# A decoder layer with a mixture of experts on one core: weights laid out in the order of their loads

## The chip, the core and the metric

The kernel runs on one core of a Trainium2 chip. The metric is the device time of one execution in microseconds; the median of three executions of the kernel before is 1303.94 us (1302.9 to 1305.6).

## What is computed

One decoder layer for 256 tokens of width 1024 in float32, then a final RMSNorm. Cut to what matters:

```
mod = silu(c) @ ada_w + ada_b                       # 1024 -> 6 x 1024
h = modulate(rmsnorm(x, norm1_g), sh1, sc1)
z = h @ w_in                                        # 1024 -> 6144
rnn_x, rnn_gate, sg_u, sg_v, g_rnn, g_sg = split(z)
y_rnn = rg_lru(conv(rnn_x), lru_wa, lru_wx, ...) * gelu(rnn_gate)
y_sg = spatial_gating(gelu(sg_u), gelu(sg_v), sg_ws, ...)
m = sigmoid(g_rnn) * (y_rnn @ w_br_rnn) + sigmoid(g_sg) * (y_sg @ w_br_sg)
x = x + gt1 * (m @ w_out)
h = modulate(rmsnorm(x, norm2_g), sh2, sc2)
# 32 experts, each token goes to 4 of them
gate, up = split(h[tok] @ w_gu[e] + b_gu[e])        # 1024 -> 2 x 1024
act = (clip(up) + 1) * gate * sigmoid(1.702 * gate)
x = x + gt2 * sum_e weight * (act @ w_down[e] + b_down[e])
out = rmsnorm(x, final_g)
```

## The kernel before

SBUF holds a pool of 24 slots of 128 partitions by 2048 float32 (8 KB per partition, 1 MiB each). Every weight passes through one of them. `want` (line 64) puts a load on a list, `stream`, in the order in which the weights are used; `pump` (line 72) issues loads from its head on SyncE's queue as long as a slot is free; `give` (line 95) frees a slot when its content has been used, and calls `pump`. So the order of the loads is fixed, and a load is late only when its slot is.

The mixer part comes first, its steps written out by hand. `ada_rows` (line 337) multiplies the first 2048 columns of ada_w, in six `PIECES`, on TensorE or VectorE; `ada_cols` and `modulate` turn the result into h. Each weight tile of w_in, w_br_rnn, w_br_sg and w_out is split by `split` (line 258) into a high part (ScalarE or VectorE) and a low part (GpSimd or VectorE), and multiplied by TensorE in three products. A weight tile is gathered from its matrix by `blocks` (line 113): rows k*128 + p of some columns, so that a partition's 8 KB come in runs of 512 columns (2 KB) or 1024 columns (4 KB); those of ada_w at the start are cut into runs of 128 or 256 columns (512 B or 1 KB), with up to four DMAs for a slot. `small_loads` (line 190) brings sg_ws and the diagonal blocks of lru_wa and lru_wx; the tile wab that takes these blocks is cleared ahead by GpSimd (line 188). GpSimd's next work is the identity matrix for the transposes (line 221).

Then the 32 experts run one after another (line 1166). Of each, eight loads of w_gu (128 rows of 2048 columns, 8 KB per partition in one run) and four of w_down (two blocks of 128 rows of 1024 columns, so two runs of 4 KB per partition) are streamed, 12 MiB per expert. TensorE gathers the tokens of the next expert, multiplies by w_gu (`up_products`, line 915) and w_down (`down`, line 935), and adds the outcome to x. `w_down` of the last expert is cut at column 384 of each half (WA) and loaded by 16 DMAs. Where an expert has more than 64 tokens, a branch (line 1228) does the rest. [...]

```
def pump():
    while at[0] < len(stream) and (left[0] or stream[at[0]][3]):
def give():
    left[0] += 1
    pump()
nc.tensor.addr_align(bass.FETCH_BLOCK_INSTRUCTIONS, offset=FETCH_SLOT, max_nops=0)
```

Of the kernel before, what the change touches and what calls it, by code (L numbers as in the profile page):

```python
# [14 lines left out]
D = 1024  # L15
# [7 lines left out]
WA = 384  # L23
BIG = 3.0e38

FETCH_SLOT = 252

LIMIT = 7.0
ALPHA = 1.702
# [7 lines left out]
PIECES = ((0,), (1,), (2, 3), (4, 5), (6,), (7,))  # L37
ROWS_ON_PE = (0, 1, 4, 5)

C_C, C_AB, C_G1, C_CW, C_CB, C_BA, C_BX, C_LAM, C_LNG, C_LNB = 0, 8, 56, 64, 96, 104, 112, 120, 128, 136  # L40
N_COLS = 144

R_G2, R_BS, R_FG = 0, 1, 2


@with_exitstack
def layer(ctx: ExitStack, tc: tile.TileContext, x, cols, rows, ada_w, ada_b, w_in, lru_wa, lru_wx,
          sg_ws, w_br_rnn, w_br_sg, w_out, w_router, b_router, w_gu, b_gu, w_down, b_down, out):
# [12 lines left out]

    stream, at, where, left, waiting, R, hooks = [], [0], {}, [NS - NU], [], {}, {}

    def want(key, src, shape, into=None):
        stream.append((key, src, shape, into))

    def new(name, dt=F32):
        assert left[0] > 0, name
# [1 line left out]
        return slots.tile([128, 2048], dt, name=name, tag="slot")  # L70

    def pump():
        while at[0] < len(stream) and (left[0] or stream[at[0]][3]):
            key, src, shape, into = stream[at[0]]
            at[0] += 1
            if into:
                w = where[into][:, 1024:]
            else:
                w = where[key] = new("_".join(str(k) for k in key))
            if len(shape) == 3:  # L80
                dst = w.rearrange("p (k a c) -> p k a c", k=shape[0], a=shape[1])
# [40 lines left out]
    for g in groups:
        for h in range(2):
            late.append((g, h, blocks(w_in, 4 * h, 4 * h + 4, col0[g], col0[g] + 512), (4, 512)))
    for nm, w in (("br", w_br_rnn), ("bs", w_br_sg)):
        for hf in range(2):
            for h in range(2):
                late.append((nm + "ab"[hf], h, blocks(w, 4 * h, 4 * h + 4, hf * 512, hf * 512 + 512), (4, 512)))
    for q in range(4):
        late.append(("out", q, blocks(w_out, 2 * q, 2 * q + 2, 0, D), (2, 1024)))  # L130
    chunks += [(g, h, shp) for g, h, src, shp in late]
    a1_src = ada_w[:, :2 * D].rearrange("(k p) (a c) -> p k a c", p=128, a=2)
    for i, kbs in enumerate(PIECES):
        n = len(kbs)
        for j in range(n):
            want(("a1", i, j), a1_src[:, j * 4:j * 4 + 8 // n, :, kbs[0] * 128:(kbs[-1] + 1) * 128], (8 // n, 2, 128 * n))
        p = kbs[0] // 2
        for kb in kbs:
            if n == 2:
                if kb % 2 == 0:  # L140
                    want(("w", p), blocks(w_in, kb, kb + 2, 0, D), (2, 1024))
            else:
                want(("w", p, "x")[:2 + kb % 2], blocks(w_in, kb, kb + 1, 0, D), (1, 1024), into=("w", p) if kb % 2 else None)
        if kbs[-1] % 2:
            want(("w", 4 + p // 2, "ga")[:2 + p % 2], blocks(w_in, 2 * p, 2 * p + 2, col0["ga"], col0["ga"] + 512),
                 (2, 512), into=("w", 4 + p // 2) if p % 2 else None)
    ada_at = {i: n for n, i in enumerate(ADA_STEPS)}
    for i in range(6, 4 + len(late) + 2):
        if i < 4 + len(late):
            want(("w", i), *late[i - 4][2:])  # L150
        if i - 4 in ada_at:
            part, kb = divmod(ada_at[i - 4], 8)
            want(("a2", ada_at[i - 4]), blocks(ada_w, kb, kb + 1, 2048 * (1 + part), 2048 * (2 + part)), (1, 2048))
# [12 lines left out]

    xv = view(new("x"), TB)
# [17 lines left out]
    wab = view(R["wab"], 16)  # L185
    rw = R["ws"][:, :1024]
    wr = selX.rearrange("p (k e) -> p k e", k=KB)
    nc.gpsimd.memset(R["wab"], 0.0)

    def small_loads():  # L190
        nc.sync.dma_start(R["ws"][0:1, 1024:], rows[R_BS:R_BS + 1])
        nc.sync.dma_start(brow, b_router)
        for h in range(2):
            nc.sync.dma_start(wsn[h], sg_ws[4 * h:4 * h + 4].rearrange("g t s -> t g s"))
        for a, w in enumerate((lru_wa, lru_wx)):
            wr_ = w.rearrange("(c h) i j -> h i c j", h=2)
            for h in range(2):
# [397 lines left out]


    def load_biases():
        bex = R["h2"][:, :1536]
        for r in range(2):
            for h in range(2):  # L600
                dst = bex[r * 64 + h * 32:r * 64 + (h + 1) * 32]
                nc.sync.dma_start(dst[:, :1024].rearrange("e (a j) -> e a j", a=2),
                                  b_gu.rearrange("e (a h j) -> e h a j", a=2, h=2)[:, h])
                nc.sync.dma_start(dst[:, 1024:], b_down[:, h * 512:(h + 1) * 512])

    def split_biases():
        bex, brs = R["h2"][:, :1536], R["brs"][:, :1536]
# [11 lines left out]
    def merge_s(hf, banks):  # L619
        for j in range(2):  # L620
# [467 lines left out]
    def rare(e):  # L1088
# [30 lines left out]
            mm(BX[h], two[:, h * 32 + e:h * 32 + e + 1].to_broadcast([128, 128]), brs[:, 1024:1536], True, False)  # L1119
        for kb in range(KB):  # L1120
            for h in range(2):
                nc.gpsimd.dma_start(wt2[n % 2], w_down[e, kb * 128:(kb + 1) * 128, h * 512:(h + 1) * 512])
# [181 lines left out]
def _layout(v):  # L1304

    import numpy as np

    v = {k: np.asarray(a) for k, a in v.items()}

    def col(a):  # L1310
        return a.reshape(-1, 128).T

    cols = np.concatenate([col(v[n].reshape(-1)) for n in
                           ("c", "ada_b", "norm1_g", "conv_w", "conv_b", "lru_ba", "lru_bx", "lru_lam",
                            "sg_ln_g", "sg_ln_b")], axis=1)
    rows = np.concatenate([v[n].reshape(1, D) for n in ("norm2_g", "sg_bs", "final_g")], axis=0)
    return {
        "x": v["x"][0], "cols": cols, "rows": rows, "ada_w": v["ada_w"][0], "ada_b": v["ada_b"],
        "w_in": v["w_in"][0], "lru_wa": v["lru_wa"][0], "lru_wx": v["lru_wx"][0], "sg_ws": v["sg_ws"][0],
        "w_br_rnn": v["w_br_rnn"][0], "w_br_sg": v["w_br_sg"][0], "w_out": v["w_out"][0],  # L1320
        "w_router": v["w_router"][0], "b_router": v["b_router"], "w_gu": v["w_gu"][0], "b_gu": v["b_gu"][0],
        "w_down": v["w_down"][0], "b_down": v["b_down"][0],
    }


# [16 lines left out]
```

## Time and profile before

| what | value |
|---|---|
| median of three executions | 1303.94 us (1302.9 to 1305.6) |
| the profiled execution | 1307.48 us, its span 1305.8 us |
| TensorE matmuls busy | 1201.8 us (92% of the span) |
| VectorE, ScalarE, GpSimd busy | 515.2, 244.6, 156.6 us |
| DMA | 472.37 MB in 112112 packets, 77092 of them under 8 KB |
| mean DMA rate over the span | 362 GB/s |
| mean granted TensorE clock | 0.972 |

The time of an execution is what the runs report; the span is the stretch from the first to the last instruction of the profile, and all times in the trace count from its start. TensorE's time is pipelined, so its busy share is not its share of peak. An idle stretch of an engine is put down to the instruction or DMA whose end released it; "issue" stands where the profile shows no releaser.

### The profile page before, as it was taken

Reading aid. Unit: us, or ns where it says so; the run is one execution under the profiler, and the core shown is the slowest. Engines: PE = TensorE matmul, PEld = TensorE weight load, DVE = VectorE, ACT = ScalarE, POOL = GpSimd, SP = SyncE. Lnnn points to the kernel's source line nnn. Section 1 sums busy time; section 2 is a strip of 40 time slices with the busy share of each in tenths; the row PEclk is TensorE's granted clock in tenths of the full one; section 3 lists DMA queues with packets and bytes.
Section 4 is the critical chain, followed back from the end, with each engine's and each line's share of the span. In section 5 each row is a group of like instructions: output and inputs, shape, how many; then the busy total and the mean of one; then the engine's idle time right before and its main releaser. Section 6 shows DMA issues by size and latency. Waiting matters only on the chain. (4 is left out here: it accounts for less than half of the span.)

```text
span 1305.8 us, 17282 instructions
## 1 busy us (share of the span) xinstructions
PE 1201.8 (92%) x6667; PEld 634.1 (49%) x6667; DVE 515.2 (39%) x866; ACT 244.6 (19%) x408; POOL 156.6 (12%) x90
## 2 busy tenths in 40 slices
PE   4798888996999999999999999999999999998996
PEld 4796888985434444434444444333333333333342
DVE  3677998674222232223222323223222222224324
ACT  3264633441200011001000110010000000001102
POOL 2543645543000000000000000000000000000000
PEclk8898989996999999999999999999999999999998
DMA  9995636976799989999999999999999999999981
GB/s 328 332 368 179 218 125 223 400 253 281 316 387 415 409 353 414 414 414 415 415 415 416 415 415 415 415 416 413 414 414 414 410 412 411 413 412 411 416 318 46
DMA packets 112112, 472.37 MB, mean 362 GB/s; under 512 B 10233, under 2 KB 27769, under 8 KB 77092
## 3 DMA queue, kind: packets, MB, share of 16 engines
q1 hardware_dynamic: 111636, 469.61, 90.7%
q8 instruction: 114, 1.87, 0.6%
q14 instruction: 90, 0.74, 0.1%
q0 software_dynamic: 272, 0.16, 0.0%
HBM read 468.68 MB, written 1.05 MB: 360 GB/s over the span
## 5 line engine op out<-in xcount | busy, mean ns | idle before, releaser
L277 PE MATMUL bank<-gu,gv 128*64 128x512 f32 (+1 forms) x2112 | 473.4, 599 | 17.1 <-DMA gu<-in_w_gu 12.4
L277 PEld LDWEIGHTS bank<-gu,gv 128*64 128x64 f32 (+1 forms) x2112 | 143.9, 136 | 307.6 <-issue 251.1
L277 PE MATMUL bank<-dn,tmp 128*64 128x512 f32 (+3 forms) x1120 | 239.0, 576 | 1.1 <-ACT tmp L982 0.3
L1012 DVE TENSOR_TENSOR x<-bank,x 128x512 f32<-128x512 f32 x124 | 79.9, 686 | 151.4 <-PE bank L277 151.4
L277 PEld LDWEIGHTS bank<-selX,h 128*128 128x128 f32 x1024 | 119.3, 195 | 40.7 <-DVE tmp L968 38.0
L277 PE MATMUL bank<-selX,h 128*128 128x128 f32 x1024 | 125.2, 281 | 13.3 <-PEq L1212 11.8
L277 PEld LDWEIGHTS bank<-dn,tmp 128*64 128x64 f32 (+1 forms) x1120 | 71.8, 135 | 132.3 <-issue 118.0
L272 POOL TENSOR_TENSOR parts<-w,parts 128x1024 fp32r<-128x1024 f32 x40 | 117.8, 2955 | 114.6 <-ACT parts L268 82.2
L277 PE MATMUL bank<-hh,parts 128*128 128x256 f32 x640 | 121.2, 300 | 8.1 <-DVE parts L272 4.2
L994 DVE TENSOR_REDUCE wsl<-bank 128x1 f32<-128x256 f32 x33 | 14.0, 425 | 286.5 <-PE bank L993 286.5
L1244 POOL DMA_DIRECT2D selX<-in_rows x4 | 2.2, 544 | 950.8 <-PE bank L277 950.8
L277 PEld LDWEIGHTS bank<-hh,parts 128*128 128x128 f32 x640 | 103.7, 205 | 11.5 <-DVE parts L272 4.6
L969 ACT ACTIVATE tmp<-tmp 128x512 f32<-128x512 f32 (+1 forms) x34 | 20.8, 611 | 466.4 <-DVE tmp L968 466.4
L277 PE MATMUL bank<-hl,parts 128*128 128x256 f32 x320 | 85.2, 297 | 0.0
L268 ACT ACTIVATE parts<-w 128x1024 fp32r<-128x1024 f32 x66 | 67.2, 1052 | 51.2 <-PE bank L277 15.5
L998 DVE SCALAR_TENSOR_TENSOR tmp<-bank,wsl,gt2h 128x512 f32<-128x512 f32 x31 | 23.3, 750 | 130.0 <-PE bank L277 130.0
L1000 ACT ACTIVATE on<-tmp 128x512 fp32r<-128x512 f32 x31 | 19.5, 629 | 262.6 <-DVE tmp L998 262.6
L277 PEld LDWEIGHTS bank<-hl,parts 128*128 128x128 f32 x320 | 61.4, 207 | 0.2 <-issue 0.2
L883 ACT ACTIVATE gv<-bank 128x512 f32<-128x512 f32 x64 | 38.3, 598 | 117.4 <-PE bank L277 117.4
L272 DVE TENSOR_TENSOR parts<-w,parts 128x1024 fp32r<-128x1024 f32 x32 | 44.4, 1396 | 27.9 <-ACT parts L268 27.8
L968 DVE TENSOR_SCALAR tmp<-bank 128x512 f32<-128x512 f32 (+1 forms) x34 | 22.7, 668 | 71.4 <-PE bank L277 71.1
L277 PE MATMUL bank<-parts,hh 128*128 128x512 f32 x128 | 42.3, 409 | 7.3 <-POOL parts L272 6.0
(229 smaller groups left out, 974.1 us busy)
## 6 DMA issues: line engine op xcount, KB each, us to landing
gu<-in_w_gu SPq DMA_DIRECT2D x256, 1024.0 KB, 19.9
dn<-in_w_down SPq DMA_DIRECT2D x124, 1024.0 KB, 20.1
w<-in_w_in SPq DMA_DIRECT2D x20, 1024.0 KB, 8.6
a<-in_ada_w SPq DMA_DIRECT2D x16, 1024.0 KB, 7.0
a<-in_ada_w SPq DMA_DIRECT2D x16, 256.0 KB, 6.7
w<-in_w_in SPq DMA_DIRECT2D x8, 512.0 KB, 7.1
a<-in_ada_w SPq DMA_DIRECT2D x8, 512.0 KB, 10.2
w<-in_w_br_rnn SPq DMA_DIRECT2D x4, 1024.0 KB, 4.9
```

The lines of the kernel that those rows point to most:

```text
L268: nc.scalar.activation(hi, w, AF.Copy)
L272: (nc.gpsimd if u in ON_POOL else nc.vector).tensor_tensor(lo, w, hi.bitcast(F32), op=OP.subtract)
L277: nc.tensor.matmul(o, a, b, start=start, stop=stop, skip_group_check=True)
L883: nc.scalar.activation(XT[:, 4 * j:4 * j + 4], bk.rearrange("p (d n) -> p d n", d=4), AF.Copy)
L968: nc.vector.tensor_scalar(gcl, g, LIMIT, None, op0=OP.min)
L969: nc.scalar.activation(sig, gcl, AF.Sigmoid, scale=ALPHA)
L994: nc.vector.tensor_reduce(w, T[:, :256], axis=mybir.AxisListType.X, op=OP.add)
L998: nc.vector.scalar_tensor_tensor(osb, o, w, g, op0=OP.mult, op1=OP.mult)
L1000: nc.scalar.activation(dst[0], osb, AF.Copy)
L1012: nc.vector.tensor_tensor(xv[:, b, c], C[h], xv[:, b, c], op=OP.add)
L1244: nc.gpsimd.dma_start(frow[q], rows[R_FG:R_FG + 1, q * 256:(q + 1) * 256])
```

## The change

The host lays out the weights in the order of the loads. `mixer_stream` lists all loads of the mixer part: for each its key, whether it fills a half of a slot, and which rows and columns of which matrix it holds. The host builds from it one array `mix` with one 1 MiB block per slot, so that a load is one DMA of 8 KB per partition in one run (4 KB for a half). w_down gets the same form (`w_dn`, `w_dn_last`), the biases become one array of 128 rows, sg_ws and w_router are turned on the host, and the recurrent blocks come as one array `lru_w` with their zeros, so that wab is not cleared. FETCH_SLOT goes from 252 to 248. No engine computes anything else.

```diff
-FETCH_SLOT = 252
+FETCH_SLOT = 248
...
+def mixer_stream():
+    late = []
+    for g in GROUPS:
+        for h in range(2):
+            late.append(("w_in", range(4 * h, 4 * h + 4), [(COL0[g], 512)]))
...
+    for i, kbs in enumerate(PIECES):
+        n = len(kbs)
+        runs = [(kbs[0] * 128, n * 128), (D + kbs[0] * 128, n * 128)]
+        for j in range(n):
+            order.append((("a1", i, j), None, "ada_w", range(j * 4, j * 4 + 8 // n), runs))
...
     def pump():
-        while at[0] < len(stream) and (left[0] or stream[at[0]][3]):
-            key, src, shape, into = stream[at[0]]
+        while at[0] < len(stream) and (left[0] or stream[at[0]][0] in where):
+            key, src, half = stream[at[0]]
             at[0] += 1
-            if into:
-                w = where[into][:, 1024:]
-            else:
-                w = where[key] = new("_".join(str(k) for k in key))
-            if len(shape) == 3:
-                dst = w.rearrange("p (k a c) -> p k a c", k=shape[0], a=shape[1])
-                for k in range(0, shape[0], 4):
-                    for a in range(shape[1]):
-                        nc.sync.dma_start(dst[:, k:k + 4, a], src[:, k:k + 4, a])
...
-            else:
-                nc.sync.dma_start(view(w, shape[0], shape[0] * shape[1]), src)
+            if key not in where:
+                where[key] = new("_".join(str(k) for k in key))
+            c0 = half * 1024 if half else 0
+            nc.sync.dma_start(where[key][:, c0:c0 + src.shape[-1]], src)
...
     for e in range(E):
         for k in range(KB):
-            want(("gu", e, k), blocks(w_gu[e], k, k + 1, 0, 2 * D), (1, 2048))
+            want(("gu", e, k), w_gu[e, k * 128:(k + 1) * 128])
         if e < E - 1:
             for k in range(4):
-                want(("dn", e, k), blocks(w_down[e], 2 * k, 2 * k + 2, 0, D), (2, 1024))
-
-    src = w_down[E - 1].rearrange("(k p) (h c) -> p k h c", p=128, h=2)
+                want(("dn", e, k), w_dn[e, k])
+
     for k in range(4):
-        want(("dn", E - 1, k), src[:, 2 * k:2 * k + 2, :, :WA], (2, 2, WA, 1))
-    want(("dn", E - 1, 4), src[:, :, :, WA:], (8, 2, 512 - WA, 1))
+        want(("dn", E - 1, k), w_dn_last[:, k * 4 * WA:(k + 1) * 4 * WA])
+    want(("dn", E - 1, 4), w_dn_last[:, 16 * WA:])
...
-    nc.gpsimd.memset(R["wab"], 0.0)
...
-        for h in range(2):
-            nc.sync.dma_start(wsn[h], sg_ws[4 * h:4 * h + 4].rearrange("g t s -> t g s"))
-        for a, w in enumerate((lru_wa, lru_wx)):
-            wr_ = w.rearrange("(c h) i j -> h i c j", h=2)
-            for h in range(2):
-                nc.sync.dma_start(wab[h * 64:(h + 1) * 64, a * 8:(a + 1) * 8, h * 64:(h + 1) * 64], wr_[h])
+        nc.sync.dma_start(R["ws"][:, :1024], sg_ws)
+        nc.sync.dma_start(R["wab"], lru_w)
...
-        nc.gpsimd.dma_start(wr, w_router.rearrange("(k p) e -> p k e", p=128))
+        nc.gpsimd.dma_start(selX, w_router)
...
-        for r in range(2):
-            for h in range(2):
...
+        nc.sync.dma_start(R["h2"][:, :1536], biases)
```

How the change moves instructions, at the places that the prediction speaks of. GpSimd's order at its start, before (wab is the tile of the recurrent blocks, ident the identity, own a copy for the expert loop):

```order
L188 MEMSET wab 128x2048
L221 ISA
L221 AFFINE_SELECT ident<-tmp 128x128
L224 AFFINE_SELECT tmp<-tmp 128x128
L226 CAST own_98<-tmp 128x128
L227 IOTA iota 128x128
L248 MEMSET selX 128x256
```

GpSimd's order at its start, with the change:

```order
L212 ISA
L212 AFFINE_SELECT ident<-tmp 128x128
L215 AFFINE_SELECT tmp<-tmp 128x128
L217 CAST own_98<-tmp 128x128
L218 IOTA iota 128x128
L239 MEMSET selX 128x256
```

The clearing of wab is gone, and the rest stands as it stood. SyncE's order at the start, before (a_ are tiles of ada_w, w_ tiles of w_in, the numbers at the end count tiles):

```order
L171 DMA colt<-in_cols 128x144
L84 DMA a_0_0_103<-in_ada_w 128x4x128 x4
L91 DMA w_108<-in_w_in 128x1024
L84 DMA a_1_0_110<-in_ada_w 128x4x128 x4
L91 DMA w_108<-in_w_in 128x1024
L91 DMA w_116<-in_w_in 128x2x512
L84 DMA a_2_0_118<-in_ada_w 128x4x256 x2
L84 DMA a_2_1_121<-in_ada_w 128x4x256 x2
L91 DMA w_124<-in_w_in 128x2x1024
```

and with the change:

```order
L167 DMA colt<-in_cols 128x144
L122 DMA a_0_0_102<-in_mix 128x2048
L122 DMA w_104<-in_mix 128x1024
L122 DMA a_1_0_106<-in_mix 128x2048
L122 DMA w_104<-in_mix 128x1024
L122 DMA w_109<-in_mix 128x1024
L122 DMA a_2_0_111<-in_mix 128x2048
L122 DMA a_2_1_113<-in_mix 128x2048
L122 DMA w_115<-in_mix 128x2048
```

The tiles come in the same order, each by one DMA with one run per partition. SyncE's order around the w_down loads of one expert in the loop, before (gu_ and dn_ are tiles of w_gu and w_down):

```order
L91 DMA gu_6_3215<-in_w_gu 128x2048
L91 DMA gu_7_3217<-in_w_gu 128x2048
...
L91 DMA dn_0_3296<-in_w_down 128x2x1024
L91 DMA dn_1_3298<-in_w_down 128x2x1024
L91 DMA dn_2_3300<-in_w_down 128x2x1024
L91 DMA dn_3_3302<-in_w_down 128x2x1024
...
L91 DMA gu_0_3373<-in_w_gu 128x2048
```

and with the change:

```order
L122 DMA gu_6_3187<-in_w_gu 128x2048
L122 DMA gu_7_3189<-in_w_gu 128x2048
...
L122 DMA dn_0_3268<-in_w_dn 128x2048
L122 DMA dn_1_3270<-in_w_dn 128x2048
L122 DMA dn_2_3272<-in_w_dn 128x2048
L122 DMA dn_3_3274<-in_w_dn 128x2048
...
L122 DMA gu_0_3345<-in_w_gu 128x2048
```

The loads stand at the same places; those of w_down have one run per partition in place of two.

## Rows read from the trace of the kernel before

**Rows 1.** Waits, 0 to 345 us: engine, line, awaited; us in total, times, longest

```profile
POOL brb L384 <- issue: 6.1, 1, 6.1
...
ACT xh L236 <- DMA x<-in_x: 2.2, 1, 2.2
...
PEld bank L277 <- DMA w<-in_w_in: 0.2, 1, 0.2
```

**Rows 2.** Busy time by stretch, first 60 us; last columns granted clock, DMA share, GB/s

```profile
0.00:20.00 20.00, 5.97 (x36) 4.39 (x36) 5.63 (x14) 8.02 (x14) 3.30 (x10) 1.00 0.97 302
20.00:40.00 20.00, 12.95 (x85) 12.01 (x86) 13.04 (x17) 4.20 (x7) 8.02 (x3) 0.81 1.09 358
40.00:60.00 20.00, 16.90 (x106) 16.70 (x107) 15.34 (x20) 6.71 (x10) 9.86 (x4) 0.77 1.06 314
```

**Rows 3.** Timeline of GpSimd at the start: start and length in us

```profile
0.79 1.81 POOL L188 MEMSET wab<- 128x2048 f32 x1 [0.29 <-POOLq L1331]
13.14 0.28 POOL L221 TENSOR_SCALAR_AFFINE_SELECT ident<-tmp 128x128 f32<-128x128 f32 x1 [10.55 <-issue]
```

**Rows 4.** Timeline of TensorE at the start

```profile
13.48 3.67 PE L326 MATMUL bank<-ident,xh 128*128 128x128 f32 x16 [13.48 <-POOL ident L221]
```

**Rows 5.** Timeline of VectorE at the start, the last part of xh

```profile
7.51 0.75 DVE L239 TENSOR_SCALAR xh<-x,st 128x1024 f32<-128x1024 f32 x1
```

**Rows 6.** Timeline of TensorE, first products of experts 1, 18 and 28

```profile
354.90 0.73 PE L277 MATMUL bank<-brs,own 128*128 128x512 f32 x2
...
849.26 0.73 PE L277 MATMUL bank<-brs,own 128*128 128x512 f32 x2
...
1156.43 0.73 PE L277 MATMUL bank<-brs,own 128*128 128x512 f32 x2
```

**Rows 7.** Waits of TensorE, 340 to 870, 870 to 1176, 1176 to 1303 us

```profile
PE bank L277 <- PEq L1212: 7.4, 19, 0.4
PE bank L277 <- PEq L1196: 2.9, 18, 0.2
...
PE bank L277 <- DMA gu<-in_w_gu: 0.6, 1, 0.6
...
PE bank L277 <- DMA gu<-in_w_gu: 11.8, 28, 0.6
...
PE bank L277 <- PEq L1279: 2.6, 1, 2.6
```

**Rows 8.** Timeline of SyncE's issues, 500 to 700 us

```profile
515.62 7.75 SPq L91 DMA_DIRECT2D dn<-in_w_down  x4
525.57 17.92 SPq L91 DMA_DIRECT2D gu<-in_w_gu  x8
545.67 9.17 SPq L91 DMA_DIRECT2D dn<-in_w_down  x4
555.65 17.95 SPq L91 DMA_DIRECT2D gu<-in_w_gu  x8
575.78 7.76 SPq L91 DMA_DIRECT2D dn<-in_w_down  x4
585.72 17.98 SPq L91 DMA_DIRECT2D gu<-in_w_gu  x8
...
695.98 2.85 SPq L91 DMA_DIRECT2D dn<-in_w_down  x2
```

**Rows 9.** Busy time by stretch in the expert loop, columns as in rows 2

```profile
355.00:361.00 6.00, 6.00 (x28) 2.12 (x30) 2.48 (x7) 0.63 (x1) 0.00 (x0) 1.00 1.01 426
366.00:373.00 7.00, 6.61 (x41) 3.46 (x38) 3.43 (x6) 0.74 (x2) 0.00 (x0) 1.00 1.03 414
500.00:870.00 370.00, 361.88 (x1844) 152.29 (x1843) 107.78 (x217) 39.23 (x76) 0.00 (x0) 1.00 1.02 415
```

**Rows 10.** DMA issues: count, KB each, median us from issue to landing

```profile
gu<-in_w_gu SPq DMA_DIRECT2D x256, 1024.0 KB, 19.9
dn<-in_w_down SPq DMA_DIRECT2D x124, 1024.0 KB, 20.1
```

More of the change, by code (lines that the diff above doesn't have):

```diff
@@ L43, with layer @@
 R_G2, R_BS, R_FG = 0, 1, 2
+def mixer_stream():
[3 more added lines that the diff above has]
+            late.append(("w_in", range(4 * h, 4 * h + 4), [(COL0[g], 512)]))
+    for w in ("w_br_rnn", "w_br_sg"):
+        for hf in range(2):
+            for h in range(2):
+                late.append((w, range(4 * h, 4 * h + 4), [(hf * 512, 512)]))
+    for q in range(4):
+        late.append(("w_out", range(2 * q, 2 * q + 2), [(0, D)]))
+    order = []
+    for i, kbs in enumerate(PIECES):
[3 more added lines that the diff above has]
+            order.append((("a1", i, j), None, "ada_w", range(j * 4, j * 4 + 8 // n), runs))
+        p = kbs[0] // 2
+        if n == 2:
+            order.append((("w", p), None, "w_in", range(2 * p, 2 * p + 2), [(0, D)]))
+        else:
+            order.append((("w", p), kbs[0] % 2, "w_in", range(kbs[0], kbs[0] + 1), [(0, D)]))
+        if kbs[-1] % 2:
+            order.append((("w", 4 + p // 2), p % 2, "w_in", range(2 * p, 2 * p + 2), [(COL0["ga"], 512)]))
+    ada_at = {i: n for n, i in enumerate(ADA_STEPS)}
+    for i in range(6, 4 + len(late) + 2):
+        if i < 4 + len(late):
+            order.append((("w", i), None, *late[i - 4]))
+        if i - 4 in ada_at:
+            part, kb = divmod(ada_at[i - 4], 8)
+            order.append((("a2", ada_at[i - 4]), None, "ada_w", range(kb, kb + 1), [(2 * D * (1 + part), 2 * D)]))
+    slots, loads = {}, []
+    for key, part, *what in order:
+        loads.append((key, part, slots.setdefault(key, len(slots)), what))
+    return loads, len(slots)
 @with_exitstack
-def layer(ctx: ExitStack, tc: tile.TileContext, x, cols, rows, ada_w, ada_b, w_in, lru_wa, lru_wx,
-          sg_ws, w_br_rnn, w_br_sg, w_out, w_router, b_router, w_gu, b_gu, w_down, b_down, out):
+def layer(ctx: ExitStack, tc: tile.TileContext, x, cols, rows, mix, ada_b, lru_w, sg_ws, w_router, b_router,
+          w_gu, w_dn, w_dn_last, biases, out):
     nc = tc.nc
@@ L62, in layer, with want @@
     stream, at, where, left, waiting, R, hooks = [], [0], {}, [NS - NU], [], {}, {}
-    def want(key, src, shape, into=None):
-        stream.append((key, src, shape, into))
+    def want(key, src, half=None):
+        stream.append((key, src, half))
     def new(name, dt=F32):
@@ L125, in layer @@
-    for nm, w in (("br", w_br_rnn), ("bs", w_br_sg)):
-        for hf in range(2):
-            for h in range(2):
[L128 to L146, printed above, removed]
@@ L147, in layer @@
-    ada_at = {i: n for n, i in enumerate(ADA_STEPS)}
[L148 to L153, printed above, removed]
+    chunks = [("x", p, (2, 1024)) for p in range(4)]
+    chunks += [(g, h, (4, 512)) for g in GROUPS + ("bra", "brb", "bsa", "bsb") for h in range(2)]
@@ L154, in layer @@
+    chunks += [("out", q, (2, 1024)) for q in range(4)]
+    ada_at = {i: n for n, i in enumerate(ADA_STEPS)}
+    for key, half, n, _ in mixer_stream()[0]:
+        want(key, mix[n] if half is None else mix[n][:, half * 1024:(half + 1) * 1024], half)
     for e in range(E):
         for k in range(KB):
-            want(("gu", e, k), blocks(w_gu[e], k, k + 1, 0, 2 * D), (1, 2048))
+            want(("gu", e, k), w_gu[e, k * 128:(k + 1) * 128])
         if e < E - 1:
             for k in range(4):
-                want(("dn", e, k), blocks(w_down[e], 2 * k, 2 * k + 2, 0, D), (2, 1024))
@@ L597, in load_biases @@
     def load_biases():
-        bex = R["h2"][:, :1536]
-        for r in range(2):
[L600 to L604, printed above, removed]
+        nc.sync.dma_start(R["h2"][:, :1536], biases)
     def split_biases():
@@ L1121, in rare @@
             for h in range(2):
-                nc.gpsimd.dma_start(wt2[n % 2], w_down[e, kb * 128:(kb + 1) * 128, h * 512:(h + 1) * 512])
+                if e < E - 1:
+                    c = (kb % 2) * 1024 + h * 512
+                    nc.gpsimd.dma_start(wt2[n % 2], w_dn[e, kb // 2, :, c:c + 512])
+                else:
+                    cA, cB = (2 * kb + h) * WA, 16 * WA + (2 * kb + h) * (512 - WA)
+                    nc.gpsimd.dma_start(wt2[n % 2][:, :WA], w_dn_last[:, cA:cA + WA])
+                    nc.gpsimd.dma_start(wt2[n % 2][:, WA:], w_dn_last[:, cB:cB + 512 - WA])
                 mm(BX[h], aX[kb // 4][:, (kb % 4) * 128:(kb % 4) * 128 + 128], wt2[n % 2], False, kb == KB - 1)
@@ L1316, in _layout @@
     rows = np.concatenate([v[n].reshape(1, D) for n in ("norm2_g", "sg_bs", "final_g")], axis=0)
-    return {
[L1318 to L1322, printed above, removed]
+    loads, n = mixer_stream()
+    mix = np.zeros((n, 128, 2048), np.float32)
+    for key, part, n, (name, ks, runs) in loads:
+        w = v[name][0].reshape(KB, 128, -1)[ks.start:ks.stop]
+        w = np.stack([w[:, :, c:c + m] for c, m in runs], axis=2).transpose(1, 0, 2, 3).reshape(128, -1)
+        c = part * 1024 if part else 0
+        mix[n, :, c:c + w.shape[1]] = w
+    lru = np.zeros((128, 2, 8, 128), np.float32)
+    for a, name in enumerate(("lru_wa", "lru_wx")):
+        w = v[name][0].reshape(8, 2, 64, 64)
+        for h in range(2):
+            r = slice(h * 64, (h + 1) * 64)
+            lru[r, a, :, r] = w[:, h].transpose(1, 0, 2)
+    w_dn = v["w_down"][0].reshape(E, 4, 2, 128, D).transpose(0, 1, 3, 2, 4).reshape(E, 4, 128, 2 * D)
+    last = v["w_down"][0, E - 1].reshape(KB, 128, 2, 512).transpose(1, 0, 2, 3)
+    gu, dn = v["b_gu"][0].reshape(E, 2, 2, 512), v["b_down"][0].reshape(E, 2, 512)
+    biases = np.concatenate([gu[:, 0], gu[:, 1], dn], axis=-1).transpose(1, 0, 2).reshape(64, 1536)
+    return {
+        "x": v["x"][0], "cols": cols, "rows": rows, "mix": mix, "ada_b": v["ada_b"],
+        "lru_w": lru.reshape(128, 2048), "sg_ws": v["sg_ws"][0].transpose(1, 0, 2).reshape(128, 1024),
+        "w_router": v["w_router"][0].reshape(KB, 128, E).transpose(1, 0, 2).reshape(128, KB * E),
+        "b_router": v["b_router"], "w_gu": v["w_gu"][0], "w_dn": w_dn,
+        "w_dn_last": np.concatenate([last[..., :WA].reshape(128, -1), last[..., WA:].reshape(128, -1)], axis=1),
+        "biases": np.concatenate([biases, biases], axis=0),
     }
```

19 lines of the change are left out of this document (4 added, 15 removed).

## The prediction, made before the changed kernel ran

> **What bounds the kernel now.** I read three views, in this order: the list of waits, to find where a load is waited for at all; the timeline of the engines at the start and in the expert loop; and the busy time by stretch with the DMA rate beside it.
>
> The mixer (to about 320 us) is not paced by its loads. In all of the first 345 us the list of waits has just two rows that name a DMA, 2.2 us for x and 0.2 us for a weight [rows 1], although the transfers of the first 60 us run at only 302 to 358 GB/s [rows 2]. The reader is to see that slow transfers are not yet a cost: the weights arrive before the splits and products that use them. What holds the start is GpSimd. It clears the tile wab for 1.81 us, then sits idle for 10.55 us, and delivers the identity matrix from 13.14 us [rows 3]; TensorE's first transposes begin at 13.48 us and are put down to that identity [rows 4], while their other input, the normalised x, is finished at 7.51 + 0.75 = 8.26 us [rows 5]. So there the chain is: clearing, GpSimd's idle stretch, identity, TensorE.
>
> The expert loop has two regimes. TensorE starts expert 1 at 354.90, expert 18 at 849.26 and expert 28 at 1156.43 us [rows 6]. The first 17 experts take 494.36 / 17 = 29.08 us each, the next ten 307.17 / 10 = 30.72 us. In the first regime TensorE waits for a load 0.6 us in all, in the second 28 times for 11.8 us, and after 1176 us the list names no DMA any more [rows 7]. Meanwhile the weight stream never stops: the 16 DMA engines are busy at a share of 1.02 [rows 9]. SyncE's first issue of a w_down run moves from 515.62 to 695.98 us over six experts [rows 8], 30.06 us for the 12 loads of 1 MiB of each. So the stream loses about 1 us per expert against TensorE's 29.08 us; TensorE eats the lead that the slots hold and from expert 18 on waits for the stream. The end is therefore set by the stream up to expert 27 or 28, and by TensorE from there on. TensorE could give back at most 307.17 - 10 x 29.08 = 16.4 us if the stream were free.
>
> **The change, part by part.**
>
> *Expert weights.* The w_gu loads keep their shape; a w_down load is the same 1 MiB, but one run of 8 KB per partition in place of two of 4 KB. The trace holds both prices. SyncE issues a load when the eighth before it has landed, so issue times show the pace of landings. From the first w_down issue to the first w_gu issue lie four landings of w_gu: 525.57 - 515.62 = 9.95, 555.65 - 545.67 = 9.98, 585.72 - 575.78 = 9.94 us [rows 8], 29.87 / 12 = 2.489 us each. Eight of those are 19.91 us, which leaves (30.06 - 19.91) / 4 = 2.537 us for a w_down load. The difference is 0.048 us. Bounds: a stretch in which w_gu alone is in flight moves 426 GB/s, one with w_down alone 414 GB/s [rows 9]; 1.0486 MB then cost 2.461 and 2.533 us, 0.072 us apart. From issue to landing, with eight loads in flight, the medians are 19.9 and 20.1 us [rows 10], 0.2 / 8 = 0.025 us apart. I take 0.048, since it comes from the pace of whole landings, and that is what TensorE waits for. The loads that count are those landing after the stream has become continuous and before the last wait: w_down of experts 2 to 26, 25 x 4 = 100 loads. That is **4.8 us** off (2.5 to 7.2), all on the path, as the waits of the second regime (16.4 us) are larger. In the first regime the same saving only makes the lead last longer; it is cashed in when the second regime comes later and lasts shorter. What is late next is TensorE itself at 29.08 us per expert.
>
> *The clearing of wab.* It goes, since the block-diagonal matrices now arrive with their zeros. GpSimd's next step is the one that sits idle for 10.55 us. If that length stays, the identity comes 1.81 us sooner, at 11.33 us, and x (8.26 us) is still ready before. I take the whole **1.8 us**; the ends are 1.8 and nothing, should the idle stretch end at a fixed time. What follows in the mixer waits for computing, so a shift of its first product is carried on; the first expert, and with it the freeing of slots that starts the expert stream, move along.
>
> [...]
>
> *Mixer weights.* The 512 B to 2 KB runs become 4 or 8 KB. I cost this at nothing: the cover is the computing ahead of every use, as shown by the absence of DMA waits. If that cover were not there, the first 60 us, in which 0.302 x 20 + 0.358 x 20 + 0.314 x 20 = 19.5 MB move [rows 2], would shrink to 47.1 us at 414 GB/s, 12.9 us.
>
> *Small loads.* lru_w grows by 0.5 MiB of zeros (about 1.3 us at 414 GB/s), the biases become one DMA in place of eight, spatial weights and router one run per partition. All lie in stretches without a DMA wait: nothing, and at most that 1.3 us if the cover were gone. The last expert's w_down loads shrink from 16 to 5; nothing waits for them, since the last waits of TensorE name branches and its own program.
>
> *Code.* TensorE's order has the same rows; only the place in a fetch block from which the expert loop is laid out moves, from slot 252 to 248. I take it as nothing; its price is with the rivals.
>
> Sum: 1.8 + 4.8 = 6.6 us. The profiled execution took 1307.48 us and would take 1300.9. It stands 3.5 us above the median of the runs, so against that median the forecast is 1303.94 - 6.6 = **1297.3 us**.
>
> **Rivals.**
>
> 1. *The length of a run does not matter above 512 B.* Then only the clearing counts: 1303.94 - 1.8 = 1302.1 us, no difference that can be told (about 0.2%, 2.6 us). For it: the mean over 500 to 870 us, 415 GB/s, is hardly above the 414 of w_down alone [rows 9], so the two prices could be those of two quiet or disturbed stretches. Against it: three cycles in a row give w_gu 2.485 to 2.495 us. [...] Chance 0.12.
>
> 2. *The start does not carry.* [...] 1303.94 - 4.8 = 1299.1 us. [...] Chance 0.14.
>
> 3. *The early loads do pace the mixer*, by waits that the list puts down to another engine. 1303.94 - 12.9 - 4.8 = 1286.2 us. Against it: two DMA rows in 345 us [rows 1]. Chance 0.04.
>
> 4. *Slower: a branch of the expert loop lands badly.* All code of the loop moves against the fetch blocks. At the branches of the loop TensorE now loses 0.2 us (L1196) and 0.4 us (L1212), but at the one of line 1279 2.6 us [rows 7]. If one branch per expert cost 2.6 us, 31 experts would pay 81 us; the 16.4 us of waits for loads would take their part of it, and 1303.94 - 1.8 + 81 - 16.4 gives about 1367 us. It decides from (16.4 + 1.8) / 31 = 0.6 us per expert. Against it: 0.2 and 0.4 us come back alike in some twenty experts whose code already lies at different places. Chance 0.07.
>
> That the change does not do what it says can be left out: the order of SyncE's queue shows one DMA of 2048 numbers per partition for each.
>
> **How the numbers follow.** My forecast has 0.63. Within it the size of the DMA step (2.5 to 7.2 us) and a us or two either way from the mixer, where TensorE's clock and the sharing between VectorE and GpSimd shift with any step, give some 1294 to 1300.5. A range from 1292.0 to 1303.0 holds the forecast, rival 2 and most of rival 1; it leaves out rivals 3 and 4 and the upper part of rival 1, some 0.16. Faster by over 0.2% (below 1301.3 us): nearly all of the forecast, rival 3 and most of rival 2, 0.75. Within 0.2%: rival 1 and the rest of these, 0.17. Slower: rival 4 and a little for disturbed clocks, 0.08.
>
> **What would show it.** After the change, the gap from the first w_down issue to the next should be 29.87 us (12 x 2.489) in place of 30.06; the identity should come at 11.3 us and the first transposes 1.8 us sooner; TensorE should still take 29.08 us per expert, reach expert 1 at about 353.1 us, and start to wait for loads some three or four experts later. The forecast is wrong if the identity stays at 13.1 us (rival 2), if the cycle stays at 30.06 us (rival 1), if expert 1 begins more than 5 us sooner (rival 3), or if an expert free of DMA waits takes over 29.6 us (rival 4).

## The result, and the profile after

The changed kernel takes 1294.12 us (median of four, 1293.0 to 1295.1); the kernel before, run beside it, 1304.77 us (1302.9 to 1308.3). The ratio is 0.9915, 95% interval [0.9892, 0.9939]: 11.1 us sooner by the ratio (8 to 14), where 6.6 were forecast. The time lies in the range, the direction is right, and both terms of the sum were too small. The profiled execution took 1294.45 us with a span of 1292.6 us, 13.2 us less than the span before.

**The start.** Timelines of GpSimd and of TensorE in the changed kernel:

```profile
10.22 0.28 POOL L212 TENSOR_SCALAR_AFFINE_SELECT ident<-tmp 128x128 f32<-128x128 f32 x1 [9.72 <-DVE cs L236]
```

```profile
10.55 3.67 PE L317 MATMUL bank<-ident,xh 128*128 128x128 f32 x16 [10.55 <-POOL ident L212]
```

The identity comes 2.92 us sooner than in [rows 3], not 1.81: besides the clearing, the idle stretch has become shorter, from 10.55 to 9.72 us. (The releaser named there, cs, ended at 9.25 us, and the identity reads nothing of it; I take the stretch as one without a releaser, as before.) The transposes follow at once, 2.93 us sooner than in [rows 4].

**The expert loop.** First products of experts 1, 23 and 28 on TensorE's timeline:

```profile
350.23 0.73 PE L268 MATMUL bank<-brs,own 128*128 128x512 f32 x2
...
989.99 0.73 PE L268 MATMUL bank<-brs,own 128*128 128x512 f32 x2
...
1141.85 0.73 PE L268 MATMUL bank<-brs,own 128*128 128x512 f32 x2
```

From 350.23 to 989.99 us lie 22 experts of 29.08 us each, without loss; in [rows 6] it was 17. The next five take 151.86 us, 6.5 us more than 5 x 29.08; before, ten experts lost 16.4. In this pair of profiles expert 28 begins 14.6 us sooner than before: 4.7 us because expert 1 begins sooner, 9.9 us because TensorE waits less for the stream. Of that, 1.4 us is given back by the end. TensorE's waits, 340 to 985 us and 985 to 1142 us (us in total, times, longest):

```profile
PE bank L268 <- PEq L1203: 8.7, 22, 0.4
PE bank L268 <- PEq L1187: 3.4, 21, 0.2
...
PE bank L268 <- DMA gu<-in_w_gu: 0.2, 1, 0.2
...
PE bank L268 <- DMA gu<-in_w_gu: 4.3, 10, 0.6
```

Against [rows 7] the DMA rows go from 0.6 and 11.8 us to 0.2 and 4.3 us. The branch rows cost per expert what they did, 0.4 and 0.2 us.

**The stream.** SyncE's issues, 500 to 700 us:

```profile
507.55 7.71 SPq L122 DMA_DIRECT2D dn<-in_w_dn  x4
517.48 17.70 SPq L122 DMA_DIRECT2D gu<-in_w_gu  x8
537.35 7.71 SPq L122 DMA_DIRECT2D dn<-in_w_dn  x4
...
686.46 7.72 SPq L122 DMA_DIRECT2D dn<-in_w_dn  x4
```

Six cycles of 12 loads take 178.91 us, 29.82 us each, where [rows 8] had 30.06. Busy time by stretch, columns as in [rows 2]:

```profile
0.00:20.00 20.00, 7.63 (x55) 5.45 (x56) 6.50 (x19) 9.49 (x17) 1.50 (x9) 0.97 0.90 352
20.00:40.00 20.00, 14.22 (x82) 13.93 (x82) 12.70 (x19) 4.11 (x7) 8.03 (x3) 0.76 1.01 416
40.00:60.00 20.00, 16.88 (x118) 16.68 (x118) 13.47 (x14) 5.89 (x8) 12.85 (x5) 0.84 1.02 419
500.00:870.00 370.00, 362.46 (x1851) 153.05 (x1849) 107.91 (x214) 39.83 (x77) 0.00 (x0) 1.00 1.01 419
```

From 20 to 60 us the loads of the mixer run at 416 to 419 GB/s in place of 358 and 314, the expert stream at 419 in place of 415 [rows 9]. The page counts 66576 packets in place of 112112, 10308 of them under 8 KB.

### The profile page after: what moved, and what is told of

Its sections match the earlier page's. It is cut to its first block, busy times and chain, and to the rows that moved or that the text cites. A ratio compares the mean times of both kernels' runs of the same rounds, so it can differ in the third digit from the quotient of the medians.

```text
span 1292.6 us, 17217 instructions
## 1 busy us (share of the span) xinstructions
PE 1201.7 (93%) x6667; PEld 637.4 (49%) x6667; DVE 515.3 (40%) x866; ACT 244.4 (19%) x408; POOL 153.8 (12%) x89
## 2 busy tenths in 40 slices
DMA packets 66576, 472.89 MB, mean 366 GB/s; under 512 B 7577, under 2 KB 7705, under 8 KB 10308
## 5 line engine op out<-in xcount | busy, mean ns | idle before, releaser
L268 PE MATMUL bank<-selX,h 128*128 128x128 f32 x1024 | 124.1, 280 | 13.3 <-PEq L1203 11.9
## 6 DMA issues: line engine op xcount, KB each, us to landing
gu<-in_w_gu SPq DMA_DIRECT2D x256, 1024.0 KB, 19.8
dn<-in_w_dn SPq DMA_DIRECT2D x124, 1024.0 KB, 19.8
```

Of the source, the lines that this page charges most:

```text
L268: nc.tensor.matmul(o, a, b, start=start, stop=stop, skip_group_check=True)
```

## The experiments

Two columns tell nearly the whole story, so all kernels that were run more than once stand in one table. *Expert 1* is its first product. *Waits* is the first product of expert 28 less that of expert 1, less 27 x 29.08 us: what TensorE lost to the stream. *Cycle* is the mean distance of first w_down issues between about 480 and 840 us (to 700 for 2 KB). A cycle is the 12 loads of one expert. The ratio has its 95% interval beside it. The transposes of b1_ident do not wait for GpSimd; its first column is their start.

| kernel | identity, us | expert 1, us | waits, us | cycle, us | ratio to before |
|---|---|---|---|---|---|
| before | 13.14 | 354.90 | 16.4 | 30.06 | 1 |
| changed | 10.22 | 350.23 | 6.5 | 29.82 | 0.9915 [0.9892, 0.9939] |
| u1_clear | 14.49 | 355.92 | 6.3 | 29.82 | 0.9953 [0.9937, 0.9968] |
| m1_late | 9.90 | 351.12 | 15.3 | 30.06 | 0.9982 [0.9970, 0.9994] |
| u3_mixer | 10.42 | 349.46 | 6.7 | 29.83 | 0.9916 [0.9894, 0.9938] |
| u2_dn4k | 10.06 | 350.78 | 13.6 | 30.09 | 0.9975 [0.9960, 0.9990] |
| d1_gu4k | 9.85 | 348.98 | 20.2 | 30.34 | 1.0046 [1.0029, 1.0063] |
| d2_dn2k | 9.74 | 349.37 | 32.2 | 30.67 | 1.0120 [1.0104, 1.0136] |
| c1_slot252 | 9.59 | 346.64 | 6.5 | 29.82 | 0.9918 [0.9899, 0.9938] |
| b1_ident | (6.88) | 345.21 | 6.4 | 29.82 | 0.9897 [0.9880, 0.9913] |

### The clearing put back (u1_clear)

```diff
+    nc.gpsimd.memset(R["wab"], 0.0)
```

> The changed kernel with one instruction put back: GpSimd clears wab ahead of its load again. Theory A (the start carries): the identity comes at least the 1.81 us of the clearing later than the 10.22 us of the changed kernel, at 12.0 us if GpSimd's idle stretch keeps its 9.35 us, at 13.1 us if it is 10.55 us again; expert 1 (350.23 us in the changed kernel) starts 1.8 to 2.9 us later and so does the end: ratio to the kernel before 0.993 to 0.994, where the changed kernel has 0.9915. Theory B (the start does not carry: the earlier expert 1 comes from the layout of the mixer's weights): the identity is late, yet expert 1 starts within 0.5 us of 350.2 us and the ratio is 0.9915 to 0.992.

Timeline of GpSimd, and TensorE's first product of expert 1:

```profile
0.78 1.80 POOL L184 MEMSET wab<- 128x2048 f32 x1 [0.29 <-POOLq L1344]
...
14.49 0.28 POOL L213 TENSOR_SCALAR_AFFINE_SELECT ident<-tmp 128x128 f32<-128x128 f32 x1 [11.91 <-issue]
```

```profile
355.92 0.73 PE L269 MATMUL bank<-brs,own 128*128 128x512 f32 x2
```

Theory A holds, and the effect is larger than it said: the identity 4.27 us later, expert 1 5.7 us later, the end 5.0 us later by the ratios (0.9953 - 0.9915 = 0.0038). The waits for the stream stay at 6.3 us. So the start carries to the end, and the stretch behind the clearing is longer, here even longer than in the kernel before.

### The clearing only moved (m1_late)

The kernel before, nothing else touched:

```diff
-    nc.gpsimd.memset(R["wab"], 0.0)
...
     nc.gpsimd.memset(selX, 0.0)
+    nc.gpsimd.memset(R["wab"], 0.0)
```

> The kernel before with one instruction moved: GpSimd clears wab behind the clearing of selX instead of as its first work; nothing else changes, no layout. Theory A (what costs is that the clearing stands ahead of GpSimd's idle stretch): the stretch starts at 0.5 us, the identity comes at 9.9 to 10.4 us instead of 13.14, expert 1 starts at 349 to 351 us instead of 354.90, and the end comes 4 to 5.3 us sooner than in the kernel before: ratio 0.996 to 0.997. Theory B (only the clearing's own 1.81 us counts): identity at 11.3 us, ratio 0.9985. Theory C (the shorter stretch of the changed kernel belongs to its fewer or longer packets): identity at 11.3 us or later, ratio 0.9985 to 1.

```profile
9.90 0.28 POOL L220 TENSOR_SCALAR_AFFINE_SELECT ident<-tmp 128x128 f32<-128x128 f32 x1 [9.40 <-DVE cs L244]
...
11.21 1.81 POOL L248 MEMSET wab<- 128x2048 f32 x1
```

```profile
351.12 0.73 PE L277 MATMUL bank<-brs,own 128*128 128x512 f32 x2
```

These are GpSimd's timeline and TensorE's first product of expert 1. The identity comes at 9.90 us and expert 1 at 351.12 us, 3.8 us sooner than before. So what cost was the place of the clearing, and neither its 1.81 us alone nor the packets. The span is 4.2 us shorter, as theory A had it; the ratio over all runs, 0.9982, is 2.3 us (0.8 to 3.9), less than it had: theory B's 0.9985 lies inside the interval, theory A's 0.997 at its end. The identity's time speaks for theory A, the size of the gain is left open between the two. So a part of the change's gain needs no new layout, only another place for one line.

### No traffic beside the stretch (s1_hold, s2_hold_clear)

```diff
+            if at[0] == 1:
+                nc.gpsimd.memset(where[key][0:1, 0:1], 0.0)
             c0 = half * 1024 if half else 0
```

with the identity made ahead of `pump`; s2_hold_clear has the clearing as well. There is one execution of each.

> The changed kernel with all weight loads held back at the start: the first of them waits for a small clearing on GpSimd that stands behind the identity, so that only x and the small columns (1.1 MB) move while GpSimd sits idle. Nothing is left out; the end will be some 5 us later, which is not the question. Theory A (GpSimd's idle stretch, 9.1 to 9.9 us without the clearing and 10.6 to 11.9 us behind it, is stretched by the transfers that run beside it): the stretch is 6 to 7.5 us, the identity comes at 6.5 to 8 us. Theory B (its length does not depend on the traffic): 9.1 to 9.9 us, identity at 9.6 to 10.4 us.

> The same with GpSimd's clearing of wab put back ahead of the identity. Theory A (traffic stretches it, and behind the clearing the stretch meets more of it): without traffic the stretch is as long as without the clearing, 6 to 7.5 us, and the identity comes 2.1 us later than there, at 8.6 to 10.1 us. Theory B (the stretch behind the clearing is longer for a reason of GpSimd's own): 10.5 us or more, identity at 13 us or later.

GpSimd's timeline without and then with the clearing:

```profile
10.33 0.28 POOL L211 TENSOR_SCALAR_AFFINE_SELECT ident<-tmp 128x128 f32<-128x128 f32 x1 [9.84 <-issue]
```

```profile
0.78 1.80 POOL L186 MEMSET wab<- 128x2048 f32 x1 [0.29 <-POOLq L1345]
10.77 0.28 POOL L212 TENSOR_SCALAR_AFFINE_SELECT ident<-tmp 128x128 f32<-128x128 f32 x1 [8.18 <-issue]
```

s1_hold came out as its theory B had it: without the clearing, the stretch has the same length with traffic (9.1 to 9.9 us) and without it (9.84). For s2_hold_clear neither theory had it: with the clearing the stretch is 8.18 us without traffic, and 10.55 and 11.91 us with it. So on a quiet start the clearing is nearly hidden from the identity (0.44 us later), as the lower end of the clearing's term (nothing, should the stretch end at a fixed time) had it; beside the weight loads it costs 2.9 to 4.3 us. The end does not show it hidden: expert 1 starts at 355.51 us with the clearing and at 353.34 us without it, and the two executions took 1298.83 and 1296.62 us, a difference that single profiles do not settle.

A stretch that begins at 0.5 us begins in little traffic, one that begins at 2.6 us beside the weight loads (the first 3 us of u1_clear move 67 GB/s, the next 3 us 378; from 6 to 9 us u1_clear moves 355 GB/s, s1_hold and s2_hold_clear none). What in the stretch depends on that, no row shows, nor why the quiet stretch is 1.7 us shorter behind the clearing (8.18 against 9.84 us). The cause stays open.

### The mixer's weights as before (u3_mixer)

`mix` is gone: ada_w, w_in, w_br and w_out are loaded by the loops of the kernel before.

```diff
-            nc.sync.dma_start(where[key][:, c0:c0 + src.shape[-1]], src)
+                for k in range(0, shape[0], 4):
+                    for a in range(shape[1]):
+                        nc.sync.dma_start(dst[:, k:k + 4, a], src[:, k:k + 4, a])
...
```

> The mixer's weights (ada_w, w_in, w_br, w_out) loaded as in the kernel before, in runs of 512 B to 2 KB, and everything else as in the changed kernel: w_down in runs of 8 KB, no clearing of wab, biases, spatial weights and router in one piece. Theory A (the mixer's loads are covered by computing): the identity comes at 11.3 us or sooner, expert 1 starts within 1 us of the changed kernel's 350.23 us and the ratio is 0.991 to 0.9925. [...]

GpSimd's timeline, TensorE's first product of expert 1, and busy time by stretch:

```profile
10.42 0.28 POOL L214 TENSOR_SCALAR_AFFINE_SELECT ident<-tmp 128x128 f32<-128x128 f32 x1 [9.92 <-issue]
```

```profile
349.46 0.73 PE L270 MATMUL bank<-brs,own 128*128 128x512 f32 x2
```

```profile
0.00:20.00 20.00, 7.43 (x60) 5.62 (x61) 6.50 (x19) 9.71 (x17) 1.50 (x9) 1.00 0.97 301
20.00:40.00 20.00, 14.20 (x94) 13.91 (x93) 14.94 (x21) 6.19 (x9) 9.76 (x4) 0.83 1.10 361
```

Theory A. The loads are as slow as before (301 and 361 GB/s against 352 and 416 in the changed kernel), the identity comes at 10.42 us all the same, expert 1 at 349.46 us, and the ratio is that of the changed kernel, 0.9916. The largest part of the diff is worth nothing that can be told here.

### The price of a run (u2_dn4k, d1_gu4k, d2_dn2k)

w_down in two runs of 4 KB; w_gu in two runs of 4 KB; w_down in four runs of 2 KB (the host arrays follow). The edit of u2_dn4k:

```diff
-            nc.sync.dma_start(where[key][:, c0:c0 + src.shape[-1]], src)
+            if len(src.shape) == 3:
+                nc.sync.dma_start(view(where[key], src.shape[0]), src.rearrange("k p c -> p k c"))
...
-                want(("dn", e, k), w_dn[e, k])
+                want(("dn", e, k), w_dn[e, 2 * k:2 * k + 2])
```

> The changed kernel with the w_down loads as they were before, two runs of 4 KB per partition. Theory A (a w_down load in two runs costs 0.048 to 0.058 us more): the cycle of 12 loads is 30.06 us again instead of 29.87, TensorE waits for loads from expert 19 or 20 on instead of 23, and the end comes 5 to 7 us later: ratio 0.995 to 0.997. Theory B (the stream gained because it started earlier and met other disturbances, and run length matters little): cycle 29.87 us, ratio 0.9915 to 0.993. Theory C (the stream pays for both, run length and its place beside the instruction fetches): cycle 30.06 us and, from about 870 us on, a pace that is another 0.9 us per expert slower, 8 to 10 us later than the changed kernel: ratio 0.9975 to 0.9995.

> The changed kernel with the w_gu loads in two runs of 4 KB per partition and the w_down loads in one of 8 KB: eight loads of each expert are split instead of the four of the kernel before, twice the dose. Theory A (each split load costs 0.048 to 0.058 us): the cycle of 12 loads is 29.87 + 8 x 0.048 = 30.25 us to 30.33 us, TensorE waits for loads from expert 15 or 16 on, and the end comes 25 x 8 x 0.048 to 0.058 = 9.6 to 11.6 us later than that of the changed kernel: ratio 0.999 to 1.0005. Theory B (run length matters little between 4 and 8 KB): cycle 29.87 us, ratio 0.9915 to 0.993.

> The changed kernel with each w_down load in four runs of 2 KB per partition instead of one of 8 KB; w_gu as it is. Theory A (each further run has the same price): two runs cost 0.27 / 4 = 0.066 us a load, so four cost three times as much, 0.20 us; the cycle of 12 loads is 29.82 + 4 x 0.20 = 30.6 us, TensorE waits for loads from about expert 13 on, and the end comes 20 to 24 us later than that of the changed kernel: ratio 1.0065 to 1.010. Theory B (it is the split itself that costs, or the first halving from 8 KB): cycle 30.1 us, ratio 0.997 to 0.9985.

SyncE's issues of w_down, first and last of the stretch that the cycle is taken from, for u2_dn4k, d1_gu4k and d2_dn2k:

```profile
509.13 9.23 SPq L123 DMA_DIRECT2D dn<-in_w_dn  x4
...
840.12 10.11 SPq L123 DMA_DIRECT2D dn<-in_w_dn  x4
```

```profile
510.17 5.22 SPq L125 DMA_DIRECT2D dn<-in_w_dn  x4
...
813.58 5.21 SPq L125 DMA_DIRECT2D dn<-in_w_dn  x4
```

```profile
510.94 16.48 SPq L123 DMA_DIRECT2D dn<-in_w_dn  x4
...
694.94 16.44 SPq L123 DMA_DIRECT2D dn<-in_w_dn  x4
```

11, 10 and 6 cycles: 30.09, 30.34 and 30.67 us. Over the 29.82 us of the changed kernel that is 0.27 us for 512 more runs per cycle (4 loads x 128 partitions), 0.52 for 1024 and 0.85 for 1536: nearly the same price for each further run, 0.065 to 0.071 us per 128 of them. The bytes moved agree: 419 GB/s in the changed kernel (500 to 870 us), 415, 411 and 407 in u2_dn4k, d1_gu4k and d2_dn2k over the stretches of these cycles. In the cycle, theory A of all three holds, slightly above its figures; u2_dn4k's theory C had the same cycle. The runs of a split load also lie in separate blocks of its array (512 or 256 KB), so their number and their places are not told apart. A 1 MiB load costs 29.82 / 12 = 2.485 us in runs of 8 KB, 0.07 us more in runs of 4 KB and 0.21 us more in runs of 2 KB.

The ends came later than theory A had for all three: u2_dn4k 7.8 us after the changed kernel (5 to 7 expected), d1_gu4k 17.1 (9.6 to 11.6), d2_dn2k 26.7 (20 to 24). In u2_dn4k that is the lower end of theory C (ratio 0.9975), which had a slower pace from about 870 us on; it comes from 900 us on. That the instruction fetches of theory C have a part in it, no run shows; the page of the changed kernel has 2.61 MB in 204 packets on its two instruction queues. The next experiment is on that surplus.

### A faster TensorE (h1_short)

```diff
         w = where["gu", e, k]
+        if s0 == 0 and 0 < e < E - 1 and k in (2, 6):
+            return
```

> The changed kernel without the w_gu products of the contraction blocks 2 and 6 in experts 1 to 30 (8 of 64 products of an expert are left out, so its output is not the layer's): TensorE then needs some 25.5 us per expert instead of 29.08 and waits for loads from expert 2 or 3 on. It asks what makes the stream lose another 0.97 us per expert (30.80 us for 12 loads instead of 29.83) from about expert 23 on in the changed kernel. Theory W (it is TensorE's waiting itself): cycles of 30.8 us from the moment the stream is continuous, at about 480 us. Theory L (something that has added up by then, whatever TensorE does): cycles of 29.83 us until 900 to 980 us, then 30.8 us. Both give a period of TensorE equal to the cycle.

SyncE's issues of w_down, 890 to 1050 us, first of the changed kernel, then of h1_short:

```profile
895.27 7.83 SPq L122 DMA_DIRECT2D dn<-in_w_dn  x4
925.16 7.71 SPq L122 DMA_DIRECT2D dn<-in_w_dn  x4
955.96 7.72 SPq L122 DMA_DIRECT2D dn<-in_w_dn  x4
985.80 8.68 SPq L122 DMA_DIRECT2D dn<-in_w_dn  x4
1016.58 8.70 SPq L122 DMA_DIRECT2D dn<-in_w_dn  x4
1047.39 8.68 SPq L122 DMA_DIRECT2D dn<-in_w_dn  x4
```

```profile
894.90 7.71 SPq L122 DMA_DIRECT2D dn<-in_w_dn  x4
924.75 7.68 SPq L122 DMA_DIRECT2D dn<-in_w_dn  x4
954.55 7.68 SPq L122 DMA_DIRECT2D dn<-in_w_dn  x4
984.34 8.32 SPq L122 DMA_DIRECT2D dn<-in_w_dn  x4
1014.77 8.69 SPq L122 DMA_DIRECT2D dn<-in_w_dn  x4
1045.57 8.69 SPq L122 DMA_DIRECT2D dn<-in_w_dn  x4
```

Theory L, in one execution. TensorE needs 25.65 us for an expert without waiting and waits for the stream long before 900 us (34.8 us from 380 to 900, where the changed kernel has 0.2):

```profile
PE bank L268 <- DMA gu<-in_w_gu: 34.8, 19, 4.2
```

yet the cycle stays at 29.8 us until 984 us and goes to 30.8 us then, about where it does in the changed kernel. So the slower cycles are the stream's own and not an answer to TensorE's waiting. With some 100 us less work on TensorE, the span is 1287.1 us, 5.5 us less than that of the changed kernel: the stream sets the end of the loop.

The onset explains the surplus. Slow cycles begin at 876 us in the kernel before, 900 in u2_dn4k, 925 (one, then from 986 on all) in the changed kernel, and 726 in d2_dn2k. In d1_gu4k the cycles alternate between 29.8 and 30.8 us until 843 us, 30.34 in the mean, and then take 31.1 in the mean. From one first w_down issue to the 22nd after it the kernel before and the changed one take

```profile
485.55 9.23 SPq L91 DMA_DIRECT2D dn<-in_w_down  x4
...
1154.62 9.19 SPq L91 DMA_DIRECT2D dn<-in_w_down  x4
```

```profile
477.72 7.72 SPq L122 DMA_DIRECT2D dn<-in_w_dn  x4
...
1139.78 7.70 SPq L122 DMA_DIRECT2D dn<-in_w_dn  x4
```

669.07 and 662.06 us: 7.0 us, made of 22 x 0.24 = 5.3 us for the runs and some 1.9 us for six slow cycles instead of eight.

What adds up until then can in part be read from the traces. Each load leaves 16 marks of completion (928 for the 58 loads of one semaphore in the changed kernel), and it has landed with the last of them. For the w_down load that the changed kernel issues at 507.55 us the last mark comes 19.8 us after the issue, the other 15 after 5.8 to 8.6 us. The last but one then comes later from cycle to cycle, and for the load of 895.27 us it has caught up, at 19.8 us; the next cycle is the first slow one. In the kernel before it goes from 11.3 us (issue at 485.55 us) to 19.7 (846.41 us), in d2_dn2k from 15.4 (510.94 us) to 19.7 (694.94 us), each time just ahead of the first slow cycle, and in h1_short from 7.6 (477.45 us) to 19.8 (984.34 us), where the slow cycles begin. So at first one late mark alone sets the pace, and the others fall behind until a second one sets it too; with split loads they start closer to the last. The bytes agree: 12 MiB in 29.82 us would be 422 GB/s, and 419 were moved, so what is issued and not yet moved grows. What a mark stands for, and why some fall behind, no run tells.

### The place of the code (c1_slot252)

```diff
-FETCH_SLOT = 248
+FETCH_SLOT = 252
```

> The changed kernel with the expert loop's code laid out from slot 252 of a fetch block, as in the kernel before, instead of 248. Theory A (the place costs nothing either way): expert period 29.08 us, ratio 0.9905 to 0.9925, the same as the changed kernel; it then also shows how well two builds of one schedule agree. Theory B (the place is part of the gain or of the loss): expert period off 29.08 us by at least 0.1 us, that is 3 us at the end, ratio off 0.9915 by at least 0.002.

Theory A: ratio 0.9918, period 29.09 us (the first two 29.19). It shows as well how far two profiles of one mixer schedule lie apart: expert 1 starts 3.6 us sooner than in the changed kernel, the identity 0.63 us sooner, and yet the ratios are the same. Single profiles do not weigh a start to better than some 3 us.

### The identity loaded (b1_ident)

```diff
-    ident = t([128, 128], "ident")
+    ident = colt[:, 144:272]
...
-    nc.gpsimd.memset(selX, 0.0)
+    nc.vector.memset(selX, 0.0)
```

> The changed kernel with the identity matrix as 128 more columns of the small input that SyncE loads behind x, and the clearing of selX on VectorE: TensorE's first transposes no longer wait for GpSimd. Theory A (after the change the identity still holds the start, and the start is carried to the end): the transposes start at 8.4 to 8.6 us, when x is normalised, instead of 10.55; expert 1 starts at 347.5 to 348.5 us instead of 350.23, and the end comes 2 to 2.8 us sooner than that of the changed kernel: ratio 0.9893 to 0.990. Theory B (with the identity at 10.2 us the weights of the mixer, or GpSimd's other start-up work, are as late): the transposes are sooner, but expert 1 starts less than 0.7 us sooner, ratio 0.991 to 0.9915.

```profile
6.88 3.68 PE L314 MATMUL bank<-colt,xh 128*128 128x128 f32 x16 [6.88 <-DVE xh L227]
```

TensorE's timeline: the transposes wait for the first half of x alone. The ratio is 0.9897, 2.3 us below the changed kernel by the ratios, as theory A had it. The transposes come sooner than its 8.4 us, and expert 1, at 345.21 us, sooner than its 347.5, by less than two profiles of one schedule differ. The intervals overlap, so that this is the fastest kernel is likely and not settled.

## Why the prediction was right, and where its sizes were wrong

*What bounds the kernel.* Right, and shown from two sides: more work for the stream (u2, d1, d2) goes to the end in full and more, less work for TensorE (h1) hardly at all.

*The clearing, 1.8 us.* Mechanism right, size too small. The step "I take the whole 1.8 us; the ends are 1.8 and nothing" left no end above the length of the instruction. The clearing also pushed the idle stretch into the weight loads: the identity moved 2.9 us here, 3.2 in m1_late, 4.3 in u1_clear, and the end 2.3 us (m1_late) to 5.0 us (u1_clear).

*Expert weights, 4.8 us.* Mechanism right, mis-sized twice. The price of a split load was read as 0.048 us and is 0.060 (30.06 against 29.82) to 0.068 us (u2_dn4k): the working took 2.489 us for a w_gu load from a stream in which split loads were always in flight; without them it is 2.485 us and the cycle 29.82 us, not 29.87. And the sum held a constant pace, while the stream has slow cycles near the end, two fewer now. Issue times show the pace of landings, as the working had it (from 480 to 1150 us the changed kernel issues a load 0.02 to 0.09 us after the eighth before it has landed, in all 202 whose landing the profile dates), but that of each load's last mark alone. Measured: 7.0 us between equal issues, 7.8 us by the ratio of u2_dn4k. The waits began five experts later than before, not three or four.

*The sum.* No two errors cancelled, both terms were too small. With 2.3 to 5.0 us for the start and 7.0 to 7.8 us for the stream, the parts make 9.3 to 12.8 us, around the 11.1 us measured.

*Mixer weights, small loads and code, nothing.* Right (u3_mixer for the first, c1_slot252 for the last; the small loads stood in u3_mixer and were not tried alone).

*Rivals.* 1 is refuted for runs of 2 to 8 KB by the three doses (0.065 to 0.071 us per 128 further runs); shorter runs, down to the 512 B of the first mixer loads, were not priced. 2 is refuted as the start carries, though an end of the stretch that is nearly fixed is what a start without traffic shows (10.33 and 10.77 us). 3 is refuted by u3_mixer: expert 1 did begin 4.7 us sooner, but just as soon with the old mixer loads. 4 did not come: the period is 29.08 us, and 29.09 us from slot 252 (c1_slot252); the fetch block stands in the kernel's code, and no view shows what a place in it does.

## What to carry to other kernels

When a stream of loads sets the end, count its runs: here each had a price of its own even at 2 to 8 KB (0.065 to 0.071 us per 128), and the pace of whole cycles in a profile gives it, taken from a kernel with one kind of load rather than from neighbours in a mixed one (0.060 to 0.068 us for a split load, where 0.048 was read). Layout work off that path can be worth nothing that a measurement shows (the mixer's loads: 0.9916 against 0.9915). A steady pace of issues need not last (29.8 us a cycle here until 986 us but for one, then 30.8): look at how far the marks of one load lie apart, not only at the last. Before removing an instruction at the start, look at what stands behind it on its engine: to move it can be worth more than its own length (the clearing of 1.81 us, and 3.2 us of the identity in m1_late).

## What the runs showed of the hardware that was not expected

- From 2 to 8 KB the price of a further run is nearly constant, 0.065 to 0.071 us per 128 runs.
- The stream slows by itself from 29.8 to 30.8 us per 12 MiB late in the kernel, at nearly the same time whether TensorE waits or not (h1_short). It does so when the last but one of a load's 16 marks has come to lie as late as the last, 19.8 us after the issue; why the marks drift stays open.
- GpSimd's idle stretch is 8.2 us long (one execution) or 10.6 to 11.9 us, by whether it begins at 2.6 us without weight traffic or beside it, and insensitive to it (9.1 to 9.9 us) when it begins at 0.5 us.
- VectorE's copy of 128x128 took 1.59 us beside GpSimd's clearing (u1_clear) and 0.23 us without it (the changed kernel):

```profile
1.08 1.59 DVE L212 CAST own<-tmp 128x128 fp32r<-128x128 f32 x1
```

```profile
1.08 0.23 DVE L211 CAST own<-tmp 128x128 fp32r<-128x128 f32 x1
```
